# Decoder trunk in fp32: gate and up of 8 of 22 SwiGLU feature tiles as seven half-size products each

## The chip, the core and the metric

The kernel runs on one core of one Trainium2 chip. The metric is the time of one execution on the device in microseconds (us). The engines are TensorE (PE in the rows, its weight loads PEld), VectorE (DVE), ScalarE (ACT), GpSimd (POOL) and SyncE (SP), whose queue issues nearly all transfers between memory and the on-chip buffers. Matmuls add into PSUM, which has eight banks of 128 partitions x 512 fp32; everything else that is computed lies in SBUF.

## The reference

Two layers of a decoder trunk over 512 tokens of width 1024, all in fp32. Each layer is a half-step SwiGLU feed-forward (FFN), a token-mixing step with three attention branches, and a second half-step FFN, each with an RMS norm before and after:

```python
def _swiglu(t, w_gate, w_up, w_down):
    return (jax.nn.silu(t @ w_gate) * (t @ w_up)) @ w_down
...
        f = _swiglu(_rmsnorm(h, ffn1_pre_g[l]), ffn1_w_gate[l], ffn1_w_up[l], ffn1_w_down[l])
        h = h + 0.5 * _rmsnorm(f, ffn1_post_g[l])
...
        f = _swiglu(_rmsnorm(h, ffn2_pre_g[l]), ffn2_w_gate[l], ffn2_w_up[l], ffn2_w_down[l])
        h = h + 0.5 * _rmsnorm(f, ffn2_post_g[l])
```

The width between up and down, D_FF, is 2816, or 22 tiles of 128 features. The change touches the four FFNs. In the names of the kernel they are a0, c0, a1 and c1: first and second FFN of layer 0, then of layer 1.

## The kernel before

**Split operands.** A matmul of full precision is made of three matmuls on rounded operands (`mm3`, L204 to L208): each operand is split into a high part, rounded by a copy on ScalarE (L180), and a low part, the rest, by a subtraction on VectorE (L181). The three are high x high, high x low, low x high. Weights arrive as fp32 blocks of 512 KB in buffers of the tag `raw` (two of them), and their parts go to the tags `wh` and `wl` (four each).

**An FFN, plain part.** The normed input lies transposed in SBUF, as high and low parts `us` with the 1024 input features on partitions (8 tiles) and 512 tokens along. Gate and up are computed with their features on partitions: a tile of 128 features is 8 x 3 matmuls of 512 columns (`gates`, `ups`). Tiles are taken in pairs, since a weight block is 512 x 256. ScalarE applies SiLU to gate out of PSUM, VectorE multiplies up by it (`hidden`, L614 to L625). The first pair is run in two halves of 256 tokens (`halved`, L629), so that it can begin before the last tokens are normed.

**An FFN, down.** For the feature tiles 0 to 7 (group 0) and 8 to 15 (group 1), down is done by Strassen's scheme in Winograd's form: hidden rows and weight are cut into 2 x 2 blocks, seven products of half the size in each direction replace eight, and the operands of some products are sums or differences of blocks (`products`, `product`, `first_factor`, L675 to L739). VectorE forms the weight differences in `BlockUnit.load` (L318 to L344) and the differences of the hidden rows in `first_factor`. The products accumulate in three sums, named by `SUM = (0, 1, 2, 0, 2, 0, 0)`: product 3, 5 and 6 go on adding to the banks of product 0, and after each of 2 to 6 the state of the banks is read out into the result block that `TO` names. The last six tiles are done plainly at the end of the FFN (`down`, L775).

**What sets the order.** One queue of jobs (`Queue`) holds for each job its weight units and a generator of matmuls. When a job starts, the weights of the next four units are split (`load_ahead`), and each split lets the next fetch go (`fetch_ahead`). The compiler's scheduler then orders each engine's instructions on that basis; engines run their queues in order. In before, the jobs of an FFN are: pair 0 and 1 halved, the pairs up to 6, and from then on the seven products of a down group placed singly between the gate and up jobs of the following pairs. The residual h stays in SBUF in four buffers of the tag `o` (eight in all) through the FFN.

## Time and profile before

| | us |
|---|---|
| median of 3 runs | 2456.08 |
| lowest and highest | 2452.51, 2456.12 |
| span of the profiled execution | 2448.5 |
| TensorE busy in it | 2432.6 |
| VectorE busy | 1550.9 |
| ScalarE busy | 1181.7 |

The profile is of one execution; its span goes from the first to the last instruction, and the difference from the median, 7.6 us, is what lies around the span. The page gives no other time of its own for that execution. In its rows, names of tiles are given without their numbers: `pgc` is a gate accumulator of c0 or c1, `pdc` one of down, `wh_uc` and `wl_uc` the parts of an up weight, `raw_dc` a fetched block of a down weight and `btc` a difference of such blocks. A row of the groups ends with the busy time, the mean ns of one instruction, and the idle time of the engine ahead of them with what ended it.

### The profile page before, as it was taken

Reading aid. Unit: us, or ns where it says so; the run is one execution under the profiler, and the core shown is the slowest. Engines: PE = TensorE matmul, PEld = TensorE weight load, DVE = VectorE, ACT = ScalarE, POOL = GpSimd, SP = SyncE. Lnnn points to the kernel's source line nnn. Section 1 sums busy time; section 2 is a strip of 40 time slices with the busy share of each in tenths; the row PEclk is TensorE's granted clock in tenths of the full one; section 3 lists DMA queues with packets and bytes.
Section 4 is the critical chain, followed back from the end, with each engine's and each line's share of the span. In section 5 each row is a group of like instructions: output and inputs, shape, how many; then the busy total and the mean of one; then the engine's idle time right before and its main releaser. Section 6 shows DMA issues by size and latency. Waiting matters only on the chain.

```text
span 2448.5 us, 31008 instructions
## 1 busy us (share of the span) xinstructions
PE 2432.6 (99%) x12167; PEld 2063.3 (84%) x12167; DVE 1550.9 (63%) x2220; ACT 1181.7 (48%) x1961; POOL 69.8 (3%) x124
## 2 busy tenths in 40 slices
PE   9999999999999999999999999999999999999998
PEld 8888889888888888888888888888888888888887
DVE  4364677678776653646644546866777866445466
ACT  4333365567655543333433333555776655333333
POOL 0000000000110000000000000000001100000000
PEclk9999999999999999999999999999999999999999
DMA  4334444222213433333424344442222243333433
GB/s 140 118 122 129 142 159 147 78 70 69 87 61 120 139 104 112 128 128 123 155 86 143 107 139 137 164 120 71 68 87 78 70 137 125 100 129 105 144 114 127
DMA packets 238598, 280.50 MB, mean 115 GB/s; under 512 B 8666, under 2 KB 188914, under 8 KB 238452
## 3 DMA queue, kind: packets, MB, share of 16 engines
q1 hardware_dynamic: 238356, 278.50, 35.5%
q8 instruction: 95, 1.56, 0.3%
q14 instruction: 51, 0.42, 0.0%
q0 software_dynamic: 96, 0.03, 0.0%
HBM read 272.20 MB, written 6.29 MB: 114 GB/s over the span
## 4 chain that ended last, share of the span: by engine, by line
PE 91%; DVE 4%; ACT 2%; DMA 1%; issue 1%; DVEq 0%; ACTq 0%
PE pg L207 3%; PE pg L206 3%; PE pg L208 3%; PE pgc L207 3%; PE puc L207 3%; PE pgc L208 3%; PE puc L208 3%; PE pgc L206 3%; PE puc L206 3%; PE pdc L207 3%; PE pdc L206 3%; PE pdc L208 3%; PE pga L206 3%; PE pga L208 3%; PE pua L208 3%; PE pga L207 3%
## 5 line engine op out<-in xcount | busy, mean ns | idle before, releaser
L206 PE MATMUL pg<-us_a,wh_wg 128*128 128x512 f32 x384 | 150.7, 392 | 0.0
L207 PE MATMUL pg<-us_a,wh_wg 128*128 128x512 f32 x384 | 149.8, 390 | 0.0
L208 PE MATMUL pg<-us_a,wl_wg 128*128 128x512 f32 x384 | 149.8, 390 | 0.0
L207 PE MATMUL pgc<-us_b,wh_gc 128*128 128x512 f32 x320 | 124.5, 389 | 0.0
L206 PE MATMUL pgc<-us_b,wh_gc 128*128 128x512 f32 x320 | 124.5, 389 | 0.0
L207 PE MATMUL puc<-us_b,wh_uc 128*128 128x512 f32 x320 | 124.5, 389 | 0.0
L208 PE MATMUL pgc<-us_b,wl_gc 128*128 128x512 f32 x320 | 124.5, 389 | 0.0
L208 PE MATMUL puc<-us_b,wl_uc 128*128 128x512 f32 x320 | 124.5, 389 | 0.0
L206 PE MATMUL puc<-us_b,wh_uc 128*128 128x512 f32 x320 | 124.5, 389 | 0.0
L181 DVE TENSOR_TENSOR wl_uc<-raw_uc,wh_uc 128x1024 fp32r<-128x1024 f32 x44 | 53.9, 1226 | 107.0 <-ACT wh_uc L180 107.0
L181 DVE TENSOR_TENSOR wl_ua<-raw_ua,wh_ua 128x1024 fp32r<-128x1024 f32 x44 | 53.8, 1225 | 98.4 <-ACT wh_ua L180 98.4
L180 ACT CAST wh_uc<-raw_uc 128x1024 fp32r<-128x1024 f32 x44 | 46.2, 1050 | 88.6 <-PE pgc L207 37.2
L181 DVE TENSOR_TENSOR wl_gc<-raw_gc,wh_gc 128x1024 fp32r<-128x1024 f32 x40 | 48.8, 1224 | 62.0 <-ACT wh_gc L180 61.7
L181 DVE TENSOR_TENSOR wl_ga<-raw_ga,wh_ga 128x1024 fp32r<-128x1024 f32 x40 | 48.8, 1224 | 61.0 <-ACT wh_ga L180 60.9
L208 PE MATMUL pda<-wh_da,ala 128*128 128x512 f32 x224 | 87.2, 389 | 0.0
L206 PE MATMUL pda<-wh_da,aha 128*128 128x512 f32 x224 | 87.2, 389 | 0.0
L208 PE MATMUL pdc<-wh_dc,alc 128*128 128x512 f32 x224 | 87.2, 389 | 0.0
L206 PE MATMUL pdc<-wh_dc,ahc 128*128 128x512 f32 x224 | 87.1, 389 | 0.0
L207 PE MATMUL pda<-wl_da,aha 128*128 128x512 f32 x224 | 87.1, 389 | 0.0
L207 PE MATMUL pdc<-wl_dc,ahc 128*128 128x512 f32 x224 | 87.1, 389 | 0.0
L208 PEld LDWEIGHTS pg<-us_a,wl_wg 128*128 128x128 f32 x384 | 72.2, 188 | 15.3
L180 ACT CAST wh_ua<-raw_ua 128x1024 fp32r<-128x1024 f32 x44 | 46.1, 1049 | 80.5 <-PE pga L207 34.1
(465 smaller groups left out, 7263.8 us busy)
## 6 DMA issues: line engine op xcount, KB each, us to landing
raw_da<-in_ffn_w_down_dram SPq DMA_DIRECT2D x58, 512.0 KB, 3.3
raw_dc<-in_ffn_w_down_dram SPq DMA_DIRECT2D x58, 512.0 KB, 3.3
raw_wg<-in_w_gate_dram SPq DMA_DIRECT2D x48, 512.0 KB, 3.5
raw_ga<-in_ffn_w_gate_dram SPq DMA_DIRECT2D x44, 512.0 KB, 3.6
raw_ua<-in_ffn_w_up_dram SPq DMA_DIRECT2D x44, 512.0 KB, 3.7
raw_gc<-in_ffn_w_gate_dram SPq DMA_DIRECT2D x44, 512.0 KB, 3.6
raw_uc<-in_ffn_w_up_dram SPq DMA_DIRECT2D x44, 512.0 KB, 3.7
raw_wo<-in_w_out_dram SPq DMA_DIRECT2D x24, 512.0 KB, 3.3
```

What stands on the lines that cost most here:

```text
L180: both = [nc.scalar.copy(h_ap, src)]
L181: make = lambda: nc.vector.tensor_tensor(l_ap, src, h_ap.bitcast(F32), ALU.subtract)
L206: nc.tensor.matmul(pt, lh, rh, start=start, stop=False, skip_group_check=free)
L207: nc.tensor.matmul(pt, lh, rl, start=False, stop=False, skip_group_check=free)
L208: nc.tensor.matmul(pt, ll, rh, start=False, stop=stop, skip_group_check=free)
```

## The change

Gate and up of feature tiles 0 to 7 are no longer computed in pairs but by the same seven-product scheme (`feature_products`, `feature_product`). The matrix of the input features (8 tiles) by the 8 feature tiles is cut into 2 x 2 blocks of 512 x 512, and the tokens into two halves of 256. A product has 4 input tiles x 4 feature tiles x 3 = 48 matmuls of 256 columns and two weight units. Of its seven products three take a block of the input as it lies in `us`, and four take sums of input blocks, which `sums` makes once per FFN while the pair 8, 9 runs. The order of the products is 0, 2, 1, 3, 4, 5, 6. Product 1 starts from a copy that ScalarE makes of the banks of product 0. After products 2 and 3 ScalarE copies the banks out, after 4 and 5 VectorE adds them to what was copied, after 1 and 6 SiLU or the multiply reads them directly.

The plan of an FFN (`PLAN`) becomes: pair 16, 17 halved; pair 8, 9 plain; seven gate products; seven up products; then the down products of group 0 between the pairs 10, 12 and 14, and those of group 1 between the pairs 18 and 20, with products 2 and 3 next to each other and products 5 and 6 at the end next to each other.

The first pair being 16, 17, its hidden rows are split at once and kept. The buffers of the residual are given up during the FFN: h is written to memory after the first pair (`leave`; for a0 the input x is there already) and fetched again before the last down tiles (`back`). Two of the freed `o` buffers become a second ring for fetched weight blocks. All weight blocks of the schemes are now fetched when used, 16 per run of seven products in place of 14; before, two blocks were kept and overwritten.

```diff
@@ BlockUnit
-        BLOCKS = ((0, 0), (1, 0), (0, 0), None, None, (0, 1), (1, 0))
-        def __init__(self, n, src, rows, k0, nk, ncol, keep, name):
+        BLOCKS = ((0, 0), (1, 0), (0, 0), (1, 1), (1, 1), (0, 0), (1, 0))
...
-            if self.n == 3:
-                tc.keep_in_program_order(self.block(self.keep.get(1, self.k0), (1, 1)))
...
+            src = raw = self.raw[:]
+            if self.n in (2, 3, 5, 6):
+                t = self.keep.get(self.k0)
+                src = raw if self.n == 5 else t
+                a, b = (t, raw) if self.n in (2, 5) else (raw, t)
+                nc.vector.tensor_tensor(src, a, b, ALU.subtract)
             self.split_from(src)
-            if self.ring():
-                self.raw = None
-                Q.fetched -= 1
-            Q.fetch_ahead()
+            self.loaded()
...
+    RINGS = {"raw": BUFS["raw"], "o": 0}
...
@@ ffn
+    NG = 2
+    ORDER = (0, 2, 1, 3, 4, 5, 6)
+    SUM = (0, 1, 2, 0, 2, 0, 0)
+    TO = ((0, 0), (0, 0), (1, 1), (0, 1), (0, 1), (1, 1), (1, 0))
+    park = [nc.dram_tensor(f"park{i}", (NT, P, D), F32, kind="Internal").ap() for i in range(2 * L)]
...
+        def leave():
+            if parked is not None:
+                for t in range(NT):
+                    nc.sync.dma_start(parked[t], hT[t][:])
+            RINGS["o"] = 2
+            Q.fetch_ahead()
+        def back():
+            new_h(f"f{name}")
+            for t in range(NT):
+                if parked is not None:
+                    nc.sync.dma_start(hT[t][:], parked[t])
+                else:
+                    nc.sync.dma_start(hT[t][:], x[0, t * P:(t + 1) * P, :])
...
+        def block(i, j, part):
+            return src.us[j][:, :, part, HALVES[i]]
+        def sums():
+            whole = lambda nm: stile([P, 4, S // 2], "f", nm + name, F32)[:]
+            tt = nc.vector.tensor_tensor
+            def fp32(i, j):
+                t = whole(f"x{i}{j}")
+                tt(t, block(i, j, 0).bitcast(F32), block(i, j, 1).bitcast(F32), ALU.add)
+                return t
+            def pair(n, t):
+                h, l = (stile([P, 4, S // 2], "o" if n == 4 else "v", f"u{x}{name}_{n}")[:] for x in "hl")
+                split(h, l, t)
+                st["u", n] = h, l
+            x21 = fp32(1, 0)
+            s = fp32(1, 1)
+            yield
+            tt(s, x21, s, ALU.add)
+            pair(2, s)
+            yield
+            x11 = fp32(0, 0)
+            tt(s, s, x11, ALU.subtract)
+            pair(3, s)
+            yield
+            tt(x11, x11, x21, ALU.subtract)
+            tt(s, block(0, 1, 0).bitcast(F32), s, ALU.subtract)
+            tt(s, s, block(0, 1, 1).bitcast(F32), ALU.add)
+            yield
+            pair(4, s)
+            yield
+            pair(5, x11)
...
+        def in_product(n):
+            if n in (0, 1, 6):
+                i, j = ((0, 0), (0, 1), None, None, None, None, (1, 1))[n]
+                return [block(i, j, part) for part in range(2)]
+            return st["u", n]
+        def feature_product(ci, up, n, uns):
+            nm = f"{name}{'gu'[up]}_{ci}_{n}"
+            if n in (0, 1, 2):
+                st["c", n] = [pbank("z" if n == 0 else "mm", f"pw{nm}_{e}") for e in range(2)]
+            if n == 1:
+                for e in range(2):
+                    nc.scalar.copy(st["c", 1][e][:], st["c", 0][e][:])
+            if n == 0:
+                if not up:
+                    st["s", ci] = {}
+            pts = st["c", SUM[n]]
+            h, l = in_product(n)
+            opens, ends = n in (0, 2), n in (1, 4, 6)
+            for un in uns:
+                for k in range(un.nk):
+                    kk = un.k0 + k
+                    for f in range(FC // 2):
+                        c = slice(f * P, (f + 1) * P)
+                        o = pts[f // 2][:, (f % 2) * S // 2:(f % 2 + 1) * S // 2]
+                        mm3(o, un.h[:, k, c], un.l[:, k, c], h[:, kk], l[:, kk], opens and kk == 0 and f % 2 == 0,
+                            ends and kk == FC // 2 - 1, free=True)
+                        yield 3 * (S // 2) * PE_US
+            if n == 0:
+                return
+            q = TO[n]
+            g = st["s", ci]
+            if not up and q not in g:
+                g[q] = stile([P, FC // 2, S // 2], "f", f"s{name}_{ci}_{q[0]}{q[1]}", F32)[:]
+            g = g[q]
+            r = hidden_rows(2 * ci + q[1])[:, :, HALVES[q[0]]] if up else g
+            for e in range(2):
+                p = pts[e][:].rearrange("p (f q) -> p f q", f=2)
+                re, ge = r[:, 2 * e:2 * e + 2], g[:, 2 * e:2 * e + 2]
+                if n in (2, 3):
+                    nc.scalar.copy(re, p)
+                elif n in (4, 5):
+                    nc.vector.tensor_tensor(re, re, p, ALU.add)
+                elif up:
+                    nc.vector.tensor_tensor(re, p, ge, ALU.mult)
+                else:
+                    nc.scalar.activation(re, p, AF.Silu)
+            if n in (4, 5):
+                if up:
+                    nc.vector.tensor_tensor(r, r, g, ALU.mult)
+                else:
+                    nc.scalar.activation(r, r, AF.Silu)
+        def feature_products(ci, up):
+            w, nm = (wu if up else wg)[l, :, ci * FC * P:(ci + 1) * FC * P], f"{'gu'[up]}{name}_{ci}"
+            keep = Keep(lambda k0: stile([P, 2, S], "o", f"t{nm}_{k0}", F32)[:])
+            for n in ORDER:
+                uns = [BlockUnit(n, w, ND // 2, k, 2, S, keep, f"{nm}_{n}_{k}", ("raw", "o")[k // 2])
+                       for k in range(0, ND // 2, 2)]
+                yield uns, (lambda n=n, uns=uns: feature_product(ci, up, n, uns))
...
@@ products
-            def make(i, k0):
-                if ci == 0:
-                    return stile([P, 2, S], "qo"[i], f"bt{name}_{i}_{k0}", F32)[:]
-                if k0 == 0:
-                    st["bt", i] = stile([P, 2, 2, S], "k", f"bt{name}_{i}", F32)
-                return st["bt", i][:, k0 // 2]
-            keep, w = Keep(make), wd[l, ci * FC * P:(ci + 1) * FC * P]
+            keep = Keep(lambda k0: stile([P, 2, S], "o", f"bt{name}_{ci}_{k0}", F32)[:])
+            w = wd[l, ci * FC * P:(ci + 1) * FC * P]
...
@@ the plan
+    PLAN = [("g", 8), ("u", 8, "sums")] + 7 * [("G", 0)] + 6 * [("U", 0)] + [("a", 0), ("U", 0), ("d", 0), ("g", 10), ("d", 0)]
+    for f in (10, 12, 14):
+        PLAN += [("u", f), ("d", 0)] + ([("g", f + 2), ("d", 0)] if f < 14 else [])
+    PLAN[-1:] = [("a", 1), ("d", 0)]
+    for f in (18, 20):
+        PLAN += [("d", 1), ("g", f), ("d", 1), ("u", f), ("d", 1)]
+    PLAN += [("d", 1)]
```

What moves on the engines, at the places that the prediction speaks of. First TensorE in a0, at the end of gate's product 5. `pwa0g_0_0_0` and `pwa0g_0_0_1` are the two banks of sum 0 for gate, `uha0_5` the high part of the input sum of product 5, `us_x_1` a half of the input itself, `pwa0u_0_0_0` the first bank of up.

```order
L206 MATMUL pwa0g_0_0_1_669<-uha0_5_649,wh_ga0_0_5_2_860 128x256
L207 MATMUL pwa0g_0_0_1_669<-ula0_5_650,wh_ga0_0_5_2_860 128x256
L208 MATMUL pwa0g_0_0_1_669<-uha0_5_649,wl_ga0_0_5_2_861 128x256
L206 MATMUL pwa0u_0_0_0_1126<-us_x_0_129,wh_ua0_0_0_0_986 128x256
L207 MATMUL pwa0u_0_0_0_1126<-us_x_0_129,wh_ua0_0_0_0_986 128x256
L206 MATMUL pwa0g_0_0_0_668<-us_x_1_130,wh_ga0_0_6_0_918 128x256
L207 MATMUL pwa0g_0_0_0_668<-us_x_1_130,wh_ga0_0_6_0_918 128x256
L208 MATMUL pwa0g_0_0_0_668<-us_x_1_130,wl_ga0_0_6_0_919 128x256
```

Product 6 follows product 5 on the same banks, with two matmuls of up's product 0 between them. Next VectorE at the same place: `tua0` is a block difference for up, `sa0_0_11` the gate block to which the banks are added (L762).

```order
L316 TENSOR_TENSOR tua0_0_0_922<-tua0_0_0_922,raw_ua0_0_2_0_924 128x1024
L181 TENSOR_TENSOR wl_ga0_0_6_0_919<-tga0_0_0_488,wh_ga0_0_6_0_918 128x1024
L762 TENSOR_TENSOR sa0_0_01_914<-sa0_0_01_914,pwa0g_0_2_0_732 128x512
L762 TENSOR_TENSOR sa0_0_01_914<-sa0_0_01_914,pwa0g_0_2_1_733 128x512
L316 TENSOR_TENSOR tua0_0_2_931<-tua0_0_2_931,raw_ua0_0_2_2_933 128x1024
L181 TENSOR_TENSOR wl_ga0_0_6_2_928<-tga0_0_2_492,wh_ga0_0_6_2_927 128x1024
L181 TENSOR_TENSOR wl_ua0_0_0_0_987<-raw_ua0_0_0_0_857,wh_ua0_0_0_0_986 128x1024
L762 TENSOR_TENSOR sa0_0_11_782<-sa0_0_11_782,pwa0g_0_0_0_668 128x512
L762 TENSOR_TENSOR sa0_0_11_782<-sa0_0_11_782,pwa0g_0_0_1_669 128x512
```

The two adds that product 6 waits for stand behind a subtraction and three low parts, two of them for up. Last, TensorE in c0 at the end of the second down group; `pdc0_1_0_0` and `pdc0_1_0_1` are the banks of its sum 0. Before, behind the last matmul of product 5:

```order
L208 MATMUL pdc0_1_0_1_9193<-wh_dc0_1_5_2_9636,alc0_1_5_9643 128x512
L206 MATMUL puc0_20_9797<-us_b0_0_7551,wh_uc0_20_0_9673 128x512
L207 MATMUL puc0_20_9797<-us_b0_0_7551,wh_uc0_20_0_9673 128x512
L208 MATMUL puc0_20_9797<-us_b0_0_7551,wl_uc0_20_0_9674 128x512
```

and with the change:

```order
L208 MATMUL pdc0_1_0_1_10193<-wh_dc0_1_5_2_10568,alc0_1_5_10575 128x512
L206 MATMUL pdc0_0_0_10804<-wh_dc0_0_0_10682,hidc0_16_8373 128x512
L207 MATMUL pdc0_0_0_10804<-wl_dc0_0_0_10683,hidc0_16_8373 128x512
L206 MATMUL pdc0_1_0_0_10192<-wh_dc0_1_6_0_10606,ahc0_1_6_10700 128x512
L207 MATMUL pdc0_1_0_0_10192<-wl_dc0_1_6_0_10607,ahc0_1_6_10700 128x512
```

Where 48 matmuls of up followed, product 6 now follows after two matmuls of the last down tiles (`pdc0_0_0`).

## The prediction

> **What bounds the kernel now.** I read the page first (engine shares, then the chain that ended last), then the table of waits for TensorE, then stretches of the timeline for its pace, then the groups by line for VectorE and the list of transfers.

> ```profile
> PE 2432.6 (99%) x12167; PEld 2063.3 (84%) x12167; DVE 1550.9 (63%) x2220; ACT 1181.7 (48%) x1961; POOL 69.8 (3%) x124
> PE 91%; DVE 4%; ACT 2%; DMA 1%; issue 1%; DVEq 0%; ACTq 0%
> ```
> ```profile
> engine line waited for: us in total, times, longest us
> PE pts L944 <- ACT ts L973: 4.8, 2, 2.4
> PE mt L860 <- DVE fa L724: 0.4, 1, 0.4
> ```

> TensorE is busy over the whole span and holds 91% of the chain. Its waits inside the four feed-forward layers (FFNs) come to next to nothing: the largest entry, 4.8 us, is in attention. So an FFN costs what its matmuls cost, and a change there is worth the matmul time it removes, less the waits it creates. A busy PE is modelled, so the price of a matmul is read from the starts of consecutive ones. First 512 columns, in an up projection, then 256 columns in the memory keys, with the same three-matmul helper:

> ```profile
> 959.66 0.39 PE L208 MATMUL puc<-us_b,wl_uc 128*128 128x512 f32 x1
> ...
> 962.84 0.39 PE L207 MATMUL puc<-us_b,wh_uc 128*128 128x512 f32 x1
> ```
> ```profile
> 370.20 0.28 PE L207 MATMUL pmk<-mn,wh_mk 128*128 128x256 f32 x1
> ...
> 375.95 0.28 PE L207 MATMUL pmk<-mn,wh_mk 128*128 128x256 f32 x1
> ```

> The first pair of rows is 14 starts apart: 3.18/14 = 0.2271 us for 512 columns. The second is 48 starts apart: 5.75/48 = 0.1198 us for 256. Half the width costs 53%, not 50%, because a fixed 12.5 ns (2 x 0.1198 - 0.2271) comes with each matmul.

> [...]

> **The change, part by part, for one FFN.**

> *Matmuls.* Removed: gate and up of 8 feature tiles, 2 x 8 tiles x 8 input tiles x 3 = 384 matmuls of 512 columns, 384 x 0.2271 = 87.2 us. Added: 2 x 7 products x 4 input tiles x 4 feature tiles x 3 = 672 of 256 columns, 672 x 0.1198 = 80.5 us. Gain 6.7 us, 26.8 us in four FFNs. The order of instructions agrees: 1152 more rows on TensorE, which is 4 x (672 - 384). An eighth of the columns goes, but the fixed part takes back a third of that. A product lasts 48 x 0.1198 = 5.75 us.

> *Three new hand-overs.* In the new sequence product 6 accumulates onto the banks of product 5 right behind it, and VectorE must first read the state after product 5. This happens for gate, for up, and at the end of the second down group, where product 6 used to stand behind a whole up projection. The nearest rows:

> ```profile
> 333.08 1.28 DVE L724 TENSOR_TENSOR fa<-fa,pda 128x512 f32<-128x512 f32 x2
> 333.82 0.42 PEld L860 LDWEIGHTS mt<-ident,mraw 128*128 128x128 f32 x4 [0.62 <-DVE fa L724]
> 333.82 1.25 PE L860 MATMUL mt<-ident,mraw 128*128 128x128 f32 x8 [0.38 <-DVE fa L724]
> ```
> ```profile
> 899.10 0.28 PE L646 MATMUL puc<-us_b,wh_uc 128*128 128x256 f32 x1
> 899.22 0.28 PE L647 MATMUL puc<-us_b,wl_uc 128*128 128x256 f32 x1
> 899.30 1.29 DVE L621 TENSOR_TENSOR hrc<-puc,sc 128x512 f32<-128x512 f32 x2 [0.74 <-PE puc L647]
> ```

> VectorE starts 0.08 us after the last 256-column matmul has started, and TensorE may go on 0.74 us after the first of the two adds has begun; the next matmul would have come after 0.12. A hand-over costs 0.70 us if VectorE is free. The second bank is no further wait: its add is done 0.6 us after the first (1.28 for two), and TensorE spends 6 x 0.12 = 0.72 us on the first bank. In the new order a few matmuls of the next job stand in the hole: two of 256 columns behind gate (0.24 us), two of 512 behind up (0.45), one or two at the end of down (0.23 to 0.45). So about 0.46 + 0.25 + 0.30 = 1.0 us per FFN is visible. That is the lower end.

> *VectorE and ScalarE in the products.* Durations:

> ```profile
> L181 DVE TENSOR_TENSOR wl_uc<-raw_uc,wh_uc 128x1024 fp32r<-128x1024 f32 x44 | 53.9, 1226 | 107.0 <-ACT wh_uc L180 107.0
> L327 DVE TENSOR_TENSOR btc<-btc,raw_dc 128x1024 f32<-128x1024 f32 x8 | 9.8, 1222 | 4.1 <-DMA raw_dc<-in_ffn_w_down_dram 4.1
> L724 DVE TENSOR_TENSOR fc<-fc,pdc 128x512 f32<-128x512 f32 x40 | 26.7, 683 | 8.5 <-PE pdc L208 8.5
> L616 ACT ACTIVATE sc<-pgc 128x512 f32<-128x512 f32 x44 | 26.1, 593 | 58.2 <-PE pgc L208 53.6 <-PE pgc L647 4.4
> L180 ACT CAST wh_uc<-raw_uc 128x1024 fp32r<-128x1024 f32 x44 | 46.2, 1050 | 88.6 <-PE pgc L207 37.2 <-PE puc L207 33.1 <-DMA raw_uc<-in_ffn_w_up_dram 12.9
> ```

> Seven products need 14 low parts at 1.23, 8 subtractions of weight blocks at 1.22, and their evacuation: for gate 4 x 0.68, for up 8 x 0.68 + 2 x 1.23, and two factors of down at 1.23. That is 29.7 us beside 40.2 us of TensorE for gate and 37.4 for up: 67 of 80.5 us, 83%. ScalarE has 30 casts at 1.05 and some 18 evacuations and SiLUs, two of them of double size, at 0.59: near 43 us. Before, the same 87.2 us of gate and up held only 16 low parts and 8 multiplies, some 25 us of VectorE. All of it stays beside TensorE, but the cover has become thin. Walking VectorE's new queue with these durations: a weight buffer comes free halfway through a product and is needed one and a half products (8.6 us) later, cast and low part take 2.3, so a product normally starts with 3 us or more in hand. The tightest place is the end of gate: the block for up's product 2 is fetched once product 5's low part is done, 5 VectorE operations and two adds must follow it (7.5 us), and the add of the hand-over stands behind them with some 0.4 us in hand. At the end of up it has about none. If VectorE is late, one operation in flight (0 to 1.2 us) is added to a hand-over. I take 0.35 for each, 1.0 per FFN.

> *The sums of the input* (12 VectorE operations, 14.7 us, and 4 casts) lie beside the second half of the first pair and the pair 8, 9: 96 x 0.12 + 96 x 0.2271 = 33 us of TensorE, with about 28 us of VectorE in all. Hidden; should that fail, the overhang of a few us would be paid once per FFN.

> *Transfers.* Each run of seven products fetches 16 blocks of 512 KB in 40 us: 8.4 MB, 208 GB/s, against 4.2 MB before. The residual is written out and read back (2 + 2 MB), and the down groups fetch 4 blocks more.

> ```profile
> raw_dc<-in_ffn_w_down_dram SPq DMA_DIRECT2D x58, 512.0 KB, 3.3
> ...
> btc<-in_ffn_w_down_dram SPq DMA_DIRECT2D x16, 512.0 KB, 4.9
> ...
> mraw<-in_mem_dram SPq DMA_DIRECT2D x4, 512.0 KB, 6.7
> ```
> ```profile
> 300.00:306.00 6.00, 6.00 (x28) 4.99 (x27) 4.06 (x4) 1.55 (x2) 0.00 (x0) 1.00 0.88 292
> ...
> 985.00:1200.00 215.00, 215.00 (x950) 178.01 (x950) 127.23 (x126) 81.26 (x89) 0.00 (x0) 1.00 0.39 130
> ```

> The last column is GB/s, the one before it the share of the queues. 292 GB/s were moved at a share of 0.88, so 208 is two thirds of what goes, and a block lands in 3.3 us alone and 4.9 in a crowd. Four buffers are in flight and a fetch starts about 9 us before its cast. I count the growth from 3.3 to 4.9 as seldom late: 0.5 us per FFN. SP's queue is in order, and behind the reloads of the residual stand the last weights of down; they have 5 us in hand.

> *The first FFN alone* has the norm of the memory input, a chain of small ScalarE and VectorE steps with table loads, in the jobs before the last hand-over. Its adds now stand behind that chain in VectorE's queue, and a transposition stands ahead of product 6 on TensorE. Its input lands 6.7 us after issue, the chain takes some 10 more, and 16 us (up of the last pair and product 5) lie over it: between 0 and 4 us, I take 2.

> Sum: -26.8 + 4 x (1.0 + 1.0 + 0.5) + 2 = -14.8 us. The profiled span of 2448.5 becomes 2433.7. The median of the runs shown is 2456.08, 7.6 above that span, for what lies around it: 2441.3.

> **Rivals.**

> *VectorE's queue becomes the bound in the products (slower).* The head of VectorE's queue is often a subtraction that waits for its block, and everything behind it waits too. For it: 83% load, in-order engine, 8 of 14 products with subtractions, and the waits for blocks that the groups show already (4.1 us in 8 subtractions of L327). Against: 3 us in hand at most places. It decides from 14.8/4 = 3.7 us more per FFN, 0.26 us per product. If each of the 8 loses the 1.6 us between 3.3 and 4.9 us but for 0.4 in hand, that is 9.6 per FFN: +38 - 15 = +24 us, 2480. With a third of it, 2454.

> *The half-wide matmuls run slower than the memory keys' (slower).* From (87.2 - 3.0)/672 = 0.1253 us a start the gain is gone. Against it: the first pair of every FFN, with 256 columns too, also runs at 0.12 (899.10 and 899.22 above). [...] At 0.130 the time is 2469.

> *The gain goes into hand-overs.* At 0.70 + 1.2 each and no cover, 5.7 us per FFN: -26.8 + 22.8 + 4 = 0: 2456, no change.

> *All hidden.* Only the 1.0 us per FFN remains: -22.8, 2433.

> **How the numbers follow.** Forecast with its neighbours down to "all hidden", 2433 to 2450: 0.70. Hand-overs eat the gain, 2451 to 2461: 0.13. VectorE bound: 0.15; slow matmuls: 0.02. A measurement of this kernel tells about 0.2% (4.9 us) from no change: faster 0.70, same 0.13, slower 0.17. The range 2433 to 2464 leaves out the strong form of the first rival and a little below.

> **What would show it.** Right: matmuls of the new products 0.12 us apart; in the table of TensorE's waits new entries for VectorE's adds in the products and in down, 12 in all, 0.3 to 1.5 us each; an FFN about 3.7 us shorter; VectorE near 80% in the products. Wrong: waits of TensorE on a low part or a cast of the product weights (VectorE or transfers bound), a pace above 0.125, or holes at the start of the products (sums late) and in the last tiles of down (reloads late).

## The result, and the profile after

The changed kernel takes 2450.96 us (median of 19 runs, 2447.53 to 2455.3), the kernel before 2456.05 us in the same session (19 runs, 2452.51 to 2459.22). The ratio is 0.9982, with a 95% interval from 0.9975 to 0.9989. So the change gains 5.1 us by the medians, where 14.8 was forecast: the sign is right, and two thirds of the gain are missing. The gain is about as large as the 0.2% (4.9 us) that the prediction took as the least that can be told from no change.

First the head of the page of the changed kernel (span; busy time, share and instructions of TensorE), and its table of TensorE's waits (engine, tile and line <- what it waited for: us in total, times, longest):

```profile
span 2447.7 us, 33939 instructions
PE 2414.5 (99%) x13319; PEld 2099.1 (86%) x13319; DVE 1750.6 (72%) x2404; ACT 1268.5 (52%) x2063; POOL 71.0 (3%) x124
```
```profile
PE pts L1064 <- ACT ts L1093: 5.5, 2, 2.9
PE mt L980 <- DVE mem_rstd L971: 2.9, 1, 2.9
PE pda L206 <- DVE fa L836: 2.4, 2, 1.5
PE utc L564 <- DVE fc L554: 1.7, 2, 1.3
PE utx L1495 <- DVE fx L1504: 1.5, 1, 1.5
PE pwa0g L206 <- DVE sa L762: 1.5, 1, 1.5
PE pwc0g L206 <- DVE sc L762: 1.5, 1, 1.5
PE uta L564 <- DVE nha L470: 1.5, 2, 1.2
PE pwc1g L206 <- DVE sc L762: 1.4, 1, 1.4
PE warm L1465 <- DVE warm L1557: 1.2, 1, 1.2
PE pwa1g L206 <- DVE sa L762: 1.1, 1, 1.1
```

The matmuls are there as counted, 1152 more than before. What is new is the table: before, its largest entry inside an FFN was 0.4 us. Now gate waits once in each FFN (four entries at L762), the second down group twice (L836), the memory's transpositions once (L980), and the norms at the borders of the FFNs are late (`utc`, `uta`). Up has no entry.

The pace and the cover in the products, in three stretches of the first FFN: the pair 8, 9 with the second part of the sums, gate up to its product 5, and gate's product 6 with up's products (us, then busy time and instructions of TensorE, its weight loads, VectorE, ScalarE, GpSimd; granted clock, share of the queues, GB/s):

```profile
37.60:59.39 21.79, 21.79 (x99) 18.02 (x97) 18.76 (x20) 9.97 (x12) 0.00 (x0) 1.00 0.76 260
```
```profile
59.39:94.00 34.61, 34.61 (x290) 34.51 (x288) 23.87 (x22) 17.68 (x21) 0.00 (x0) 1.00 0.59 180
95.97:136.15 40.18, 40.18 (x334) 40.18 (x335) 30.68 (x29) 20.82 (x24) 0.00 (x0) 1.00 0.39 121
```

288 matmuls in 34.61 us are 0.1202 us each, forecast 0.1198. VectorE is busy for 69% and 76% of the two runs of products, where 83% was forecast, and the sums, VectorE at 86%, cost TensorE nothing. Within the products, then, the pace is the forecast one and VectorE keeps up.

**A ledger.** From the starts of neighbouring matmuls the lost time can be added up: what a start comes later than the pace of its width, as a wait where it is over 0.3 us, as a late start where it is between 0.06 and 0.3 us (a matmul at half clock comes 0.1 to 0.2 us late). The traces record the granted clock, so late starts can be split by it. The hole at the memory's transpositions is taken from the table of waits. The first column is the forecast. The second is the mean over three profiled executions of the changed kernel (spans 2447.7, 2447.4 and 2450.0) less that of two of the kernel before (2448.5 and 2452.0), from 20 us on:

| us | forecast | measured |
|---|---|---|
| matmuls: 2688 x 0.1202 less 1536 x 0.2271 | -26.8 | -25.8 |
| waits at gate's product 6 (4 x) | 3.2 | 6.8 |
| waits at up's product 6 (4 x) | 2.4 | none above 0.3 |
| waits at product 6 of the second down group, without the first FFN | 2.6 (all four) | 2.1 |
| end of the first FFN: memory's norm, and product 6 behind it | 2.0 | 4.2 |
| transfers; measured as waits at the norms and memory products | 2.0 | 3.3 |
| other waits | 0 | 1.2 |
| late starts at half clock | 0 | 4.3 |
| late starts at full clock | 0 | 2.2 |
| sum | -14.8 (from unrounded parts) | -1.7 |

Of the 4.3 us at half clock, 2.0 lie behind the hole at the end of the first FFN, 1.9 behind gate's waits and the rest in attention. The 2.2 us at full clock are some 23 starts more that come about 0.1 us late; what delays them no run here isolates. The mean spans differ by 1.9 us, so the ledger closes. The runs differ by 5.1: time and span lie 1.8 us apart (2449.47 and 2447.7 in the first profile of the changed kernel, 2453.74 and 2452.0 in e9 of the kernel before), so the median run of the kernel before has a span near 2454.3, above both of its profiled ones. What it loses there no trace shows.

### The profile page after: what moved, and what is told of

It is laid out like the page before. It is cut to its first block, busy times and chain, and to the rows that moved or that the text cites. A ratio compares the mean times of both kernels' runs of the same rounds, so it can differ in the third digit from the quotient of the medians.

```text
span 2447.7 us, 33939 instructions
## 1 busy us (share of the span) xinstructions
PE 2414.5 (99%) x13319; PEld 2099.1 (86%) x13319; DVE 1750.6 (72%) x2404; ACT 1268.5 (52%) x2063; POOL 71.0 (3%) x124
## 4 chain that ended last, share of the span: by engine, by line
PE 51%; DVE 4%; DMA 2%; ACT 2%; issue 1%; DVEq 0%; ACTq 0%
PE pdc L206 3%; PE pdc L208 3%; PE pdc L207 3%; PE pg L206 2%; PE pg L207 2%; PE pg L208 2%; PE pgc L207 2%; PE puc L206 2%; PE pgc L206 2%; PE pgc L208 2%; PE puc L208 2%; PE puc L207 2%; PE pda L206 1%; PE pda L208 1%; PE pda L207 1%
## 5 line engine op out<-in xcount | busy, mean ns | idle before, releaser
L207 PE MATMUL pg<-us_a,wh_wg 128*128 128x512 f32 x384 | 149.9, 390 | 0.0
L208 PE MATMUL pg<-us_a,wl_wg 128*128 128x512 f32 x384 | 149.7, 390 | 0.0
L181 DVE TENSOR_TENSOR wl_uc<-raw_uc,wh_uc 128x1024 fp32r<-128x1024 f32 x44 | 53.8, 1223 | 64.6 <-ACT wh_uc L180 64.5
L181 DVE TENSOR_TENSOR wl_ua<-raw_ua,wh_ua 128x1024 fp32r<-128x1024 f32 x44 | 53.7, 1222 | 59.9 <-ACT wh_ua L180 59.8
L180 ACT CAST wh_dc<-raw_dc 128x1024 fp32r<-128x1024 f32 x50 | 52.6, 1051 | 82.5 <-DMA raw_dc<-in_ffn_w_down_dram 37.3
L180 ACT CAST wh_da<-raw_da 128x1024 fp32r<-128x1024 f32 x50 | 52.4, 1049 | 73.0 <-DMA raw_da<-in_ffn_w_down_dram 22.6
L207 PE MATMUL pda<-wl_da,aha 128*128 128x512 f32 x224 | 88.1, 393 | 0.0
L208 PE MATMUL pda<-wh_da,ala 128*128 128x512 f32 x224 | 88.0, 393 | 0.0
L181 DVE TENSOR_TENSOR wl_dc<-raw_dc,wh_dc 128x1024 fp32r<-128x1024 f32 x50 | 61.1, 1223 | 37.0 <-ACT wh_dc L180 36.5
L208 PE MATMUL pdc<-wh_dc,alc 128*128 128x512 f32 x224 | 87.2, 389 | 0.0
L207 PE MATMUL pdc<-wl_dc,ahc 128*128 128x512 f32 x224 | 87.2, 389 | 0.0
L208 PEld LDWEIGHTS pg<-us_a,wl_wg 128*128 128x128 f32 x384 | 72.3, 188 | 15.4
L206 PEld LDWEIGHTS pg<-us_a,wh_wg 128*128 128x128 f32 x384 | 72.6, 189 | 14.4
L181 DVE TENSOR_TENSOR wl_da<-raw_da,wh_da 128x1024 fp32r<-128x1024 f32 x50 | 61.1, 1223 | 33.0 <-ACT wh_da L180 32.4
L207 PEld LDWEIGHTS pg<-us_a,wh_wg 128*128 128x128 f32 x384 | 72.4, 189 | 14.3
L184 DVE SCALAR_TENSOR_TENSOR wl_wg<-raw_wg,wh_wg 128x1024 fp32r<-128x1024 f32 x48 | 58.7, 1222 | 31.7 <-ACT wh_wg L183 31.4
L206 PE MATMUL pgc<-us_b,wh_gc 128*128 128x512 f32 x192 | 74.7, 389 | 0.0
L207 PE MATMUL pgc<-us_b,wh_gc 128*128 128x512 f32 x192 | 74.7, 389 | 0.0
L208 PE MATMUL pgc<-us_b,wl_gc 128*128 128x512 f32 x192 | 74.7, 389 | 0.0
## 6 DMA issues: line engine op xcount, KB each, us to landing
raw_da<-in_ffn_w_down_dram SPq DMA_DIRECT2D x74, 512.0 KB, 3.5
raw_dc<-in_ffn_w_down_dram SPq DMA_DIRECT2D x74, 512.0 KB, 3.6
raw_ga<-in_ffn_w_gate_dram SPq DMA_DIRECT2D x56, 512.0 KB, 4.3
raw_ua<-in_ffn_w_up_dram SPq DMA_DIRECT2D x56, 512.0 KB, 4.1
raw_gc<-in_ffn_w_gate_dram SPq DMA_DIRECT2D x56, 512.0 KB, 4.0
raw_uc<-in_ffn_w_up_dram SPq DMA_DIRECT2D x56, 512.0 KB, 3.9
raw_wg<-in_w_gate_dram SPq DMA_DIRECT2D x48, 512.0 KB, 3.7
raw_wo<-in_w_out_dram SPq DMA_DIRECT2D x24, 512.0 KB, 3.6
```

Of the source, the lines that this page charges most:

```text
L180: both = [nc.scalar.copy(h_ap, src)]
L181: make = lambda: nc.vector.tensor_tensor(l_ap, src, h_ap.bitcast(F32), ALU.subtract)
L184: make = lambda: nc.vector.scalar_tensor_tensor(l_ap, src, scale, h_ap.bitcast(F32), ALU.mult, ALU.subtract)
L206: nc.tensor.matmul(pt, lh, rh, start=start, stop=False, skip_group_check=free)
L207: nc.tensor.matmul(pt, lh, rl, start=False, stop=False, skip_group_check=free)
L208: nc.tensor.matmul(pt, ll, rh, start=False, stop=stop, skip_group_check=free)
```

## The experiments

Theory H: the hand-overs at gate are dearer than forecast. Theory M: the memory's norm, uncovered in the first FFN. Theory K: the clock behind the waits. Rivals: D, VectorE as the bound, so that a wait removed returns elsewhere; R, the reload of the residual; Q, that the half-wide products themselves bring less. Ratios are to the kernel before, measured beside each; 0.001 is 2.5 us. The changed kernel stands at 0.9982.

**e1: another order of the products**

```
-    ORDER = (0, 2, 1, 3, 4, 5, 6)
+    ORDER = (0, 2, 3, 1, 5, 4, 6)
```

with the copy of product 0's banks for product 1 moved up to product 2.

> The seven products of gate and up in the order 0, 2, 3, 1, 5, 4, 6, so that no product accumulates onto the banks of the one just before it. After the change TensorE waits for the adds of product 5 of gate 1.63, 1.63, 1.26 and 1.58 us in the four FFNs, 6.1 us in all. Theory H (these hand-overs are part of the missing gain): the four waits go, 5 to 6 us less than the changed kernel, about 2445 us. Rival D (VectorE's queue is the bound in the products): VectorE is late at the next place, the waits reappear at another product, less than 2 us gained, 2449 to 2451 us.

Measured 2442.38 us, ratio 0.9946 (0.9933 to 0.996): 0.0036 below the changed kernel, 8.8 us. In its table of waits the four entries of gate are gone, and those of the down group and of the memory stay:

```profile
PE mt L981 <- DVE mem_rstd L972: 3.1, 1, 3.1
PE pda L206 <- DVE fa L837: 2.9, 2, 2.0
...
PE pwa1u L208 <- DVE wl_ua L181: 0.7, 1, 0.7
```

H holds, and D falls in the main: the one wait that came in place of 6 us is of 0.7 us, though late starts at full clock are 2.0 us more than in the changed kernel's mean. The gain is larger than gate's waits; see e14.

**e8: without the memory's statistic**

```
-                ss = mem_rstd[:, t]
-                nc.scalar.activation(mn[t][:, 0:D // M], ..., AF.Square, accum_out=ss[:, 0:1])
...
+                nc.gpsimd.memset(mem_rstd[:, t], 1.0)
```

> Leaves out the statistic of the memory's norm (square, sums, logarithm, exponential and correction of the first FFN; GpSimd writes ones in its place), so the memory input isn't normalised. Theory M (in the changed kernel the norm's chain makes the hole of 2.9 us in the first FFN and the hole the 12 matmuls at half clock, 2.4 us): 4 to 5.5 us below the changed kernel, 2445 to 2447 us. Rival V (the copies of the small vectors, moved to the same place, are as late): the wait only changes its releaser, less than 1.5 us, 2449.5 to 2451 us.

Measured 2441.12 us, ratio 0.9948 (0.9936 to 0.9961): 8.4 us below the changed kernel, more than M expected (4 to 5.5). The wait `mt` is gone from its table, and what it left of the hand-over is

```profile
PE pda L206 <- DVE fa L836: 0.7, 1, 0.7
```

where the changed kernel has 2.4 in two. The end of the first FFN runs 6.6 us ahead: the matmul of the plain down that starts at 336.53 us in the changed kernel starts at 329.93 here. The waits at the norms and memory products are 0.6 us shorter than the changed kernel's mean of 6.4.

What the statistic does there is to be read on ScalarE and in SP's queue of the changed kernel. ScalarE (start, us, line, operation, out<-in):

```profile
318.10 1.28 ACT L967 ACT_TABLE_LOAD   x1
319.39 0.20 ACT L967 ACTIVATE mem_rstd<-mem_rstd 128x1 f32<-128x1 f32 x1
319.61 1.28 ACT L968 ACT_TABLE_LOAD   x1
320.91 0.20 ACT L968 ACTIVATE mem_rstd<-mem_rstd 128x1 f32<-128x1 f32 x1
321.02 1.03 ACT L180 CAST wh_da<-bta 128x1024 fp32r<-128x1024 f32 x1
321.95 0.61 ACT L180 CAST hida<-sa 128x512 fp32r<-128x512 f32 x1
322.58 1.28 ACT L617 ACT_TABLE_LOAD   x1
323.88 1.05 ACT L180 CAST wh_da<-raw_da 128x1024 fp32r<-128x1024 f32 x1
```

SP's queue:

```profile
317.51 0.37 SPq L250 DMA_DIRECT2D raw_da<-in_ffn_w_down_dram  x1
...
326.23 0.38 SPq L250 DMA_DIRECT2D raw_da<-in_ffn_w_down_dram  x1
```

TensorE:

```profile
325.06 0.47 PE L980 MATMUL mt<-ident,mraw 128*128 128x128 f32 x1 [2.93 <-DVE mem_rstd L971]
325.19 0.77 PE L206 MATMUL pda<-wh_da,hida 128*128 128x512 f32 x1
326.85 0.79 PE L206 MATMUL pda<-wh_da,aha 128*128 128x512 f32 x1 [0.89 <-DVE fa L836]
327.44 0.63 PE L207 MATMUL pda<-wl_da,aha 128*128 128x512 f32 x1
```

For each row of the memory the statistic is a pass over the row (1.06 us, ahead of these rows) and two small operations of 0.2 us, each behind a table load of 1.28 us; a fifth load, at L617, follows them. The casts of the last weights stand behind, so the weight buffers stay full: SP's queue waits 6.5 us at one place for the low part of such a weight, and the next fetch is issued 8.7 us after the one before (in e8 the same two stand 6.0 us apart, 315.75 and 321.76). TensorE waits 2.9 us for the statistic, 1.4 by its starts (0.89 of it idle) for the add of product 5, which stands in VectorE's queue behind the same chain, and then runs at half clock: start to start 0.43 us instead of 0.23, as the stretch shows:

```profile
322.00:332.00 10.00, 6.18 (x16) 4.44 (x17) 7.33 (x14) 4.02 (x7) 0.00 (x0) 0.66 0.64 235
```

The kernel before had the same chain, but its rows of the memory were fetched at 299.72 and 300.12 us, here at 305.27 and 307.09, and an up projection of 10.9 us lay between product 5 and what needs it. No run takes the chain out of the kernel before; there the memory's transpositions wait 0.4 us.

**e2: an up projection between products 5 and 6 of the second down group; e5: with e1; e6: with e5, and the small vectors elsewhere**

```
-    PLAN += [("d", 1)]
+    PLAN[-2:] = [("d", 1), ("u", 20), ("d", 1)]
```
```
             for what in plan:
+                if what == ("G", 0) and name == "a0" and what not in made:
+                    Q.add([], vectors)
...
-        if name == "a0":
-            Q.add([], vectors)
```

> In the second down group the up projection of tiles 20, 21 stands between products 5 and 6 instead of ahead of 5; products 4 and 5, which use different banks, are neighbours in its place. In the profile of the changed kernel the first FFN loses 2.9 us to the norm of the memory input, 1.4 us to the hand-over behind it and 2.4 us to 12 matmuls at half clock; the third FFN loses 1.6 us to the hand-over. Theory M (the norm's chain has too little cover where product 6 follows product 5 directly, and the hole pulls the clock down): nearly all of it comes back, 7 to 8 us, about 2443 us. Rival: the chain is late because its input is fetched 6 to 7 us later than before, and an up projection more over it does not hide it: 2 to 3 us gained, 2448 us.

> The order of products of e1 and the plan of e2 together. Theories H and M: the gains add, 12 to 14 us below the changed kernel, 2437 to 2439 us. Rival D: with the waits of the hand-overs gone VectorE is late elsewhere, 6 to 8 us in all, 2443 to 2445 us.

> e5 with the job of the small vectors (two transpositions and two copies of ScalarE) ahead of the products of the first FFN, as the kernel before had it ahead of its down products, instead of right ahead of the memory's transpositions. In e5 a transposition of the memory input still waits 3.7 us, now for ScalarE's copy of those vectors, which stands behind a cast that waits for its weights, and some matmuls behind it run at half clock. Theory V (the moved job of the vectors holds the hole open): the wait and the slow matmuls go, 4 to 6 us below e5, 2434 to 2436 us. Rival M (the norm's own chain is as late): the wait changes its releaser to the norm and stays, less than 1.5 us, 2438 to 2440 us.

Measured: e2 2448.48 us, ratio 0.9975 (0.9964 to 0.9987), 1.7 us below the changed kernel; e5 2439.56, 0.9934 (0.9921 to 0.9946), 2.9 below e1 and 11.8 below the changed kernel, a little under the 12 to 14 of its theory; e6 2439.87, 0.9941 (0.9929 to 0.9954), no gain over e5. The hand-over of the third FFN is cured, but the hole in the first is not. It only changes its name. In e2, then e5, then e6 (e6's profile is of its slowest run, 2443.21 us, so its hole may be larger than usual):

```profile
PE mt L980 <- ACT nbgate L128: 3.0, 1, 3.0
```
```profile
PE mt L981 <- ACT nbgate L128: 3.7, 1, 3.7
```
```profile
PE mt L981 <- DVE fa L837: 5.7, 2, 5.2
```

First the copies of the small vectors, then, with these out of the way, VectorE's adds. In e5 the copy (331.13 us) stands behind a cast that waited 1.08 us for its weights, until 330.12; in e6 the add (332.43) stands behind the low part of such a cast (1.20 us, until 330.21). The two casts ahead, whose buffers the fetches wait for, start only at 323.53 and 323.49, right behind four table loads of 1.28 us. So the rival of e2 was right about the time, and e6's theory V fell; its rival had the time (2438 to 2440 us), but not the reason, since it named the norm as the releaser. The releaser of a wait names the last in a line; here three different ones stood at the end of the same line, and of the changes tried up to here only taking away its head (e8) closed the hole.

**e10 to e13: the statistic early**

```
+        if name == "a0":
+            Q.add([], mem_stats)
         for what in plan:
```

with a job that loads the two rows a first time, and takes both logarithms, then both exponentials; the chain at the end keeps only the scaling. e11 is e5 with it, e12 e6 with it, e13 e1 with it.

> The changed kernel, with the statistic of the memory's norm computed ahead of gate 8, from a load of its own, and with both rows' logarithms and exponentials side by side; at the end of the FFN only the scaling is left. Nothing is left out. Theory S (that statistic stands in ScalarE's queue ahead of the casts of the last weights, the weight buffers come free late, and the whole end of the first FFN and the start of the memory's projections is late): as without the statistic, 8 to 10 us below the changed kernel, 2441 to 2443 us. Rival (the chain needs its place anyway and delays the sums of the input or the products instead): 0 to 4 us gained, 2447 to 2451 us.

> e5 (order of products and plan) with the early statistic. Theory S: the gain of e1 (8 us) and that of the statistic (9 us) add, with about 1 us for the hand-over of the second down group: 18 us below the changed kernel, 2432 to 2435 us. Rival: the statistic and the plan cure the same stall, and the small vectors' copies still hold the transpositions: 2436 to 2438 us.

> e11 with the small vectors ahead of the products. Theory S: with the casts in time the vectors cost nothing where they were, so no difference to e11 beyond 1 us. Rival V (the vectors' copies wait on their own behind casts): 2 to 4 us below e11.

> The order of products of e1 and the early statistic, without the plan of e2, so the hand-over of the second down group stays (0.7 to 1.6 us in the first and third FFN). Theories H and S: 2 us above e11, 2434 to 2437 us. Rival: the plan of e2 costs as much elsewhere as it saves, no difference to e11.

Measured: e10 2445.15 us, ratio 0.996 (0.9946 to 0.9973), 5.4 us below the changed kernel, between theory and rival; e11 2438.08, 0.9926 (0.9913 to 0.994); e12 2437.25, 0.9928 (0.9916 to 0.9941); e13 2441.69, 0.9945 (0.9933 to 0.9957), no gain over e1 and 4.7 us above e11, where its theory had 2. The wait `mt` is gone in e10, but the early chain costs a part: the second half of the first pair waits for its input, 1.1 us in e12:

```profile
PE pga L639 <- ACT us_x L183: 1.1, 1, 1.1
```

and in e10 and e13 product 6 still follows product 5 directly: in e13 its wait is 2.1 us with 1.7 of late starts behind, so what the statistic gave back there went into the hand-over. e11 and e12 are the shortest of the kernels that leave nothing out, 18 us below the kernel before, with no difference between the two that can be told, as e12's theory had it; e11 was forecast 3 to 6 us faster than it is, and its rival's upper end, 2438 us, fits.

**e16: e5 without the statistic**

> e5 (order of products and plan) without the statistic of the memory's norm, so the memory input isn't normalised. Theory (the gate's hand-overs and the stall behind the statistic are two separate losses): e1 brought 8.6 us and leaving out the statistic 9.5 us, together about 18 us below the changed kernel, 2432 to 2434 us. Rival (they overlap, or share the chance of the half clock, so that each alone brought more than its share): 12 to 15 us, 2436 to 2439 us.

Measured 2436.04 us, ratio 0.9912 (0.9895 to 0.9928): 0.0070 below the changed kernel, 17.2 us, to within some 4 us. e1 brought 8.8 and e8 8.4, and e2's plan, which is in e16 too, 1.7 by itself: within the interval they add up. The time lies at the lower end of the rival's range, and the interval doesn't exclude the rival's 15 us. That these are two separate losses is told by the traces: e1 keeps the wait `mt` at 3.1 us, and e8 keeps gate's four waits, of 0.9 to 1.9 us.

**e4: without reading the residual back**

```
-                if parked is not None:
-                    nc.sync.dma_start(hT[t][:], parked[t])
...
+                nc.gpsimd.memset(hT[t][:], 0.5)
```

> Leaves out the reading back of the residual: GpSimd fills its four tiles with a constant in place of four DMAs of 512 KB, so the output lacks the residual of each FFN. Theory R (the reload in SP's queue delays the last weights behind it, ScalarE waits for them, and the norms at the end of the FFNs come 1 to 2.5 us later): the waits of the transpositions behind the first FFN (1.4 and 0.7 us) and at the start of the third FFN (1.4 us) go, 3 to 5 us less than the changed kernel, 2446 to 2448 us. Rival (the order of VectorE's queue makes the norms late): no change, 2450 to 2452 us.

Measured 2450.6 us, ratio 0.9982 (0.9973 to 0.9991): no change. R falls as a cause in the time. In its trace the norm at the start of the third FFN is no longer as late (`utc` 1.1 us in two instead of 1.7), but `uta` behind the first FFN waits 1.9 instead of 1.5.

**e7: plain pairs under the new plan**

```
-    PLAN = [("g", 8), ("u", 8, "sums")] + 7 * [("G", 0)] + 6 * [("U", 0)] + [("a", 0), ("U", 0), ("d", 0), ...
+    PLAN = [("g", 8), ("u", 8)] + [(x, f) for f in (0, 2, 4) for x in "gu"] + [("g", 6), ("a", 0), ("u", 6), ("d", 0), ...
```

> The changed kernel with gate and up of the 8 tiles as plain pairs again and without the sums of the input; the new order of the plan, the parked residual and the new place of the vectors stay. Theory P (the products bring what the sum of matmuls says, and the rest of the change costs): 26.8 us of matmuls come back and the four waits of gate, 6.1 us, go: 20 us above the changed kernel, 2470 to 2473 us, so 15 us above the kernel before. Rival Q (the rest of the change costs nothing and the products bring only what the result shows): as the kernel before, 2455 to 2458 us.

Measured 2459.72 us, ratio 1.0023 (1.0013 to 1.0032): 10 us above the changed kernel, 6 above the kernel before, so between P and Q. The plan, the parking and the new place of the vectors cost 6 us together; the hole at the end of the first FFN, the half clock behind it and 0.9 us at the third FFN are in its trace too. Its profile (a span of 2460.7, from a run above the median) lies 12.3 us above the mean span of the changed kernel. Of the 25.8 us of matmuls the products so keep less than half: against e7 they take back 6.8 in gate's waits, 1.3 at the statistic, 2.5 in waits at the norms and memory products, 1.0 in other waits and 1.5 in late starts.

**e9, e14, e15: more profiles of both kernels**

> The kernel before once more, for another profiled execution: the first one had a span of 2448.5 us at a granted clock of 0.999, while the spans of 16 runs beside the experiments lie between about 2450 and 2456.6 us at 0.997 to 0.999. Theory C (the first profile was a lucky one, and the rest differ by matmuls at half clock behind waits in attention): a span of 2451 to 2456 us, with the same waits of TensorE and the difference in stretches where the granted clock is below 1. Rival: the same clock and more waits for transfers.

> The changed kernel once more, for another profiled execution. Its runs lie in two groups, near 2449 and 2453 us. Theory K (each wait of TensorE over 1 us is at times followed by 3 to 4 us at half clock, by chance): the same waits at the same places within 0.3 us, and a span that differs from 2447.7 us by the number of half-clock stretches, about 1.5 us each. Rival: the waits themselves differ between executions, by late transfers.

> As e14, a third profiled execution of the changed kernel. Theory K: a span within 6 us of the first, the difference in half-clock stretches behind the same waits. Rival: the waits themselves differ by more than 1 us.

The kernel before: span 2452.0 us. C holds in the span and falls in its reason: the late starts are the same 12.2 us as in the first profile (12.3); 3.2 us more went into waits at the norms behind the second and third FFN, the first of them

```profile
PE utc L584 <- DVE fc L574: 1.7, 2, 1.1
```

The changed kernel: spans 2447.4 and 2450.0, waits mostly of the same names. The waits themselves move by up to 1.4 us (gate of the last FFN 1.4, 1.5 and 2.8), more than K allowed, so both K and its rival have a part. Where K is seen best is behind gate's wait in the first FFN: in the first profile at full clock, in e15 at half clock, with a wait of 1.6 us right ahead in both:

```profile
96.00:100.00 4.00, 4.00 (x33) 4.00 (x34) 1.65 (x2) 1.98 (x2) 0.00 (x0) 1.00 0.96 317
```
```profile
97.40:101.40 4.00, 3.95 (x21) 3.95 (x22) 1.73 (x2) 1.06 (x1) 0.00 (x0) 0.59 0.93 327
```

21 matmuls instead of 33 in the same 4 us. Over the seven profiles with gate's four waits (the changed kernel three times, e2, e4, e8, e10), 9 of 28 such waits, of 1.1 to 3.0 us, are followed by 16 or 17 matmuls at half clock, some 3.4 us, of which 1.5 us are lost.

Which of them are followed can be read from the record of the clock. In each of the 17 profiles the falls of the clock lie whole multiples of 3.413 us apart (in the first profile of the changed kernel five falls lie 93, 84, 355 and 182 of them apart, to within 0.2 us), and it stays at half for one or two stretches of 3.413 us (the last one ends with the program). So an execution can be cut into windows of 3.413 us with every recorded fall at a border. If one adds up by how much TensorE's starts come late within one window, the 9 waits lie in windows that lost 2.00 to 2.49 us, and the 19 others in windows that lost at most 1.94. A wait of 3.0 us in e15 that a border splits into 1.7 and 1.3 is not followed. The first gate wait of e15 shares its window with a wait of 0.5 us for a cast: 2.35 us lost, TensorE busy for 1.59 of 3.41. In the first profile of the changed kernel 1.83 us are lost there, and TensorE is busy for 1.94. So what K called chance goes, in these profiles, with where the borders fall and what else is lost in the same window. The limit near 2 us is read from these 28 waits and not tested by a run.

With 1.9 us at half clock in an average profile of the changed kernel, gate's hand-overs cost 6.8 + 1.9 = 8.7 us, and e1 brought 8.8. That the two are so close is partly luck: in e1's profile other waits are 1.1 us less than in the changed kernel's mean, half clock is 2.5 less, and late starts at full clock are 2.0 more.

## Why the prediction was wrong

The missing 9.7 us lie in three terms of the sum. Gate's hand-overs were counted at 3.2 us and cost 8.8 (e1). The first FFN alone was counted at 2.0 us and cost 8.4 (e8); both costs are known to within some 4 us. The half clock behind such waits was put at nothing, without a reason, and has a part in both. The 2.4 us for up went the other way.

- **Matmuls.** Right: 0.1202 us a start for 0.1198, 25.8 us for 26.8. The rival of slower half-wide matmuls falls.
- **Three new hand-overs, and VectorE's lateness.** Two steps failed here, in opposite directions. At gate it was the "0.4 us in hand" and the 0.35 us taken for an operation in flight. The place and the mechanism were right, the size not: 0.8 us a wait was counted, and 1.3 to 1.6 came, once 3.0. A low part for up stands right ahead of the add in VectorE's fixed order (of the three low parts listed ahead of it, this one is for up and two are for gate's product 6), so a whole operation is paid, not a share of one (weight loads and one matmul left out):

```profile
93.82 0.28 PE L208 MATMUL pwa0g<-uha,wl_ga 128*128 128x256 f32 x1
94.00 0.38 PE L206 MATMUL pwa0u<-us_x,wh_ua 128*128 128x256 f32 x1
94.11 1.22 DVE L181 TENSOR_TENSOR wl_ua<-raw_ua,wh_ua 128x1024 fp32r<-128x1024 f32 x1
95.24 1.27 DVE L762 TENSOR_TENSOR sa<-sa,pwa0g 128x512 f32<-128x512 f32 x2
95.97 0.39 PE L206 MATMUL pwa0g<-us_x,wh_ga 128*128 128x256 f32 x1 [1.47 <-DVE sa L762]
```

  The add could have gone at 93.90, 0.08 us after the last matmul. VectorE comes free at 94.11, takes the low part first, and starts the add at 95.24: 1.34 us late, 1.13 of them the low part. The 0.73 us from the add's start to TensorE's next is the forecast 0.74. VectorE had waited 3.56 us for a fetched block of up's weights until 88.36 and then worked without a break until the add: the operations that the working put at 7.5 us took 6.9, but began too late. That the low part costs 1.13 us is read from the rows; no run moves it alone, or fetches the block sooner.

  At up the price of a hand-over was too high. A low part, for down, stands ahead of the add there too (other rows left out; `hra` is the block of hidden rows that the add goes to):

```profile
134.80 1.22 DVE L181 TENSOR_TENSOR wl_da<-raw_da,wh_da 128x1024 fp32r<-128x1024 f32 x1
135.94 1.27 DVE L762 TENSOR_TENSOR hra<-hra,pwa0u 128x512 f32<-128x512 f32 x2
136.03 0.28 PE L208 MATMUL pwa0u<-uha,wl_ua 128*128 128x256 f32 x1
136.15 0.40 PE L206 MATMUL pda<-wh_da,aha 128*128 128x512 f32 x1
136.67 0.39 PE L206 MATMUL pwa0u<-us_x,wh_ua 128*128 128x256 f32 x1
```

  The first add starts 0.09 us before the last matmul of product 5, in this FFN and, within 0.01 us, at all twelve ends of up in the three profiles. It needs only the first of the two banks, whose last matmul starts six matmuls, 0.72 us, earlier. The prediction counted its 0.70 us from the last matmul of the product. Product 6 again follows 0.73 us after the add, and the two matmuls pulled ahead cover that: no wait above 0.3 us, where 2.4 was counted in four. Over the eleven hand-overs other than the one at the end of the first FFN the two errors cancel in good part, by luck (8.9 us of waits, 7.6 counted).
- **The first FFN alone.** Taken as 2 us, between 0 and 4; measured 4.2 in waits with 2.0 at half clock behind them, and 8.4 us by taking the chain away. The working asked only when the statistic's result is there. It didn't ask what stands behind its table loads on ScalarE: the casts of the last weights, whose buffers hold up SP's queue (6.5 us at one place) and so the last transfers; plain down comes 6.6 us later than in e8.
- **Nothing for the clock.** Missing altogether: 4.3 us at half clock, and beside it 2.2 us of late starts at full clock. Each wait was priced by its own length. The rows of the kernel before show the half clock too, in the second attention, behind a wait of 2.6 us (1.4 us of late starts; granted clock 0.52 from 1821.0 to 1824.5).
- **The sums, and transfers within the products.** Right for TensorE: of the products' weights it waits for one cast in one of three profiles (0.5 us). VectorE's own wait for a block, 3.56 us ahead of the end of gate, has a part in the lateness there. Transfers and norms at the borders were counted at 2.0 and came to 3.3.
- **The level.** 7.6 us were set between span and time; it is 1.8, and the first profile of the kernel before was shorter than its median run by the rest. This didn't touch the forecast of the difference.

Of the rivals, "the gain goes into hand-overs" came nearest in time. Its mechanism, 1.2 us of lateness at every hand-over, holds at gate alone; the rest of the loss came from the statistic and the clock. The first rival's mechanism is seen in the block that VectorE waits for ahead of the end of gate (3.56 us in the first FFN, 3.01 in the last); as a bound on the products it falls. Of the 12 new waits named as a sign of being right six came, four at gate and two in down. The holes in the last tiles of down were named as a sign that the prediction fails, and there one was, though not by late reloads (e4).

## What to carry to other kernels

Price a new wait of TensorE at its length and look in the profiles for half clock behind such waits: here 9 of 28 had it, 1.5 us each, all in windows of 3.413 us that lost 2.00 us or more. Read the engine's fixed order for what stands ahead of the releasing operation, since a whole operation can be paid (1.13 us at gate here), and ask which bank that operation needs first. When a step moves closer to its user, look at what queues behind it on its own engine, table loads above all (1.28 us each here), and follow the weight buffers from there. When a wait changes its releaser as you cure it, look for the head of the line.
